# A transformer block with seven-product multiplications: the additions of the heads' raw weight blocks go from GpSimd to VectorE

## The chip, the cores and the metric

One core of a Trainium2 chip. A core has five engines that run their own instruction queues in order: TensorE (PE, the matrix products; its weight loads are listed apart as PEld), VectorE (DVE), ScalarE (ACT), GpSimd (POOL) and SyncE (SP, here only a queue for DMAs). The metric is the time of one execution in microseconds (us) on the device; lower is better.

## What is computed

One layer of a diffusion transformer block for a sequence of 2048 tokens of width 1024, with 256 context tokens. Cut to what matters:

```python
hx = rmsnorm(x, norm1_g) * (1 + sc1) + sh1             # the same for ctx -> hc
p  = hx @ w_in                                         # 1024 x 4608, split into heads of 128 columns:
#   4 gated (HGRN2) heads: query, value, forget gate of both directions, output gate
#   4 retention heads:     query, key (both with a 2d rotary embedding), value, gate
mix = bidirectional chunk scans of the 8 heads, started from the context's states
x  = x + g1 * (mix @ w_out)
hx2 = rmsnorm(x, norm2_g) * (1 + sc2) + sh2
gate, up = split(hx2 @ w_up)                           # 2 x 2816 columns
x  = x + g2 * ((silu(conv3(gate)) * up) @ w_down)
return rmsnorm(x, final_g)
```

## The kernel before

**Products.** All large matrix products are made in float16 pairs: a float32 operand is scaled by a power of two and written as a float16 value and its float16 rest, and three products of TensorE (lines 88 to 90) stand for one. On top of that the products are blocked two by two and made with seven block products instead of eight. For that the operand on the left is turned into seven sums and differences of its four blocks.

**Weights of a head.** `head_weights(h)` (line 692) gives, for each head, two pairs of column groups of `w_in` (for heads 0 to 6: "z" with the gates, or key and query, and "vg" with value and gate; for head 7 the pair "z" alone, since its value and gate are single). Each pair is loaded into two tiles `raw` of 128x8x128 float32. ScalarE squares both (L718) for the scale, a small matrix product sums over the partitions, and a handful of 128x1 instructions of VectorE (L99 to L103, L684 to L689) make a power of two of it. Then `pair_blocks` (line 668) makes the seven blocks: for each one, ScalarE writes the scaled float16 value (L674) and VectorE the rest (L675, which reads that value and the raw block). The blocks beyond the four raw ones come from `left_blocks` (line 511), in place, by four additions or subtractions of 128x512 float32, which this file calls "additions":

```python
        emit(3, a22)
        add(a22, a21, a22, ALU.add)          # line 519
        yield
        emit(4, a22)
        add(a21, a11, a21, ALU.subtract)     # line 522
        yield
        emit(6, a21)
        add(a11, a22, a11, ALU.subtract)     # line 525
        yield
        emit(5, a11)
        add(a12, a12, a11, ALU.subtract)     # line 528
        yield
        emit(2, a12)
```

`emit` is the pair of L674 and L675. `add` is the function handed in by the caller. There are 2 x 7 + 1 = 15 pairs over the eight heads, so 60 additions of this kind, named `raw<-raw` in the profile.

**Two other users.** `up_weights` (line 1494) does the same, by `pair_blocks`, for the 22 pairs of `w_up` (named `wur<-wur`), and `act_pairs` does it for activations, by `left_blocks` directly (`act<-act`).

**What runs beside it.** While one group of 512 tokens of a head goes through its scan (`hg_sweep1`, line 839, for the gated heads; `ret_sweep1`, line 1226, for retention), the projections of the next group are woven in between (`hg_proj`, `ret_proj`). The next head's weights are worked out by a list of items, a few of which are taken up at two points of each group (`tick`). VectorE's large pieces in the scans are the products on K and Q by the running gates (L874, L879; L759 multiplies neighbouring gates) and, for retention, the rotary embedding (L1200, L1222, L1223). GpSimd has, beside the additions, the sum of K over both directions (L824), one half of the rotary product (L1199) and the small reciprocal roots of the norms (L71 to L76). During the first three retention heads the remaining modulation rows are summed up on VectorE as well (`macc`, L301, L303).

**Order of the work.** The program is written as one sequence. A planner orders it when the program is made, with a model of every instruction's duration, and fixes the order in which each engine's queue holds its instructions; semaphores between engines follow from the tiles that are read and written. Nothing is ordered by hand around the additions.

Of the kernel before, what the change touches and what calls it, by code (L numbers as in the profile page):

```python
# [50 lines left out]
def view(t, off, dims):  # L51
    return bass.AP(t.tensor, t.offset + off, [t.ap[0]] + dims)


class Kern:
# [609 lines left out]
        yield  # L665


    def pair_blocks(self, raws, W, s, neg):

        nc = self.nc  # L670

        def emit(m, v):
            sc = neg if m == 3 else s
            nc.scalar.activation(W[m][:, 0], v, AF.Copy, scale=sc)  # L674
            nc.vector.scalar_tensor_tensor(W[m][:, 1], v, sc, W[m][:, 0], ALU.mult, ALU.subtract)  # L675
        blocks = [r[:, 4 * c:4 * c + 4] for r in raws for c in range(2)]
        yield from self.left_blocks(blocks, emit, nc.gpsimd.tensor_tensor)

    def scales(self, total, dqx, tag):

# [11 lines left out]
    def head_weights(self, h):  # L692

        if h < NH:
            want = [("z", "z", (1024 + h * P, 1536 + h * P)), ("q", "q", (h * P,)), ("vg", "vg", (512 + h * P, 2048 + h * P))]
        else:
            o = (h - NH) * P
            want = [("z", "z", (3072 + o, 2560 + o))]
            vg = (3584 + o, 4096 + o)
            want += [("vg", "vg", vg)] if h < 2 * NH - 1 else [("v", "vg", vg[:1]), ("g", "vg", vg[1:])]  # L700
        nc = self.nc
        src = self.I["w_in"][0].rearrange("(k p) n -> p k n", p=P)
        W, items = {}, []
        for nm, tag, cols in want:
            raws, st = [], {}

            def load(cols=cols, raws=raws, tag="ou2" if h == 0 and nm == "q" else "wr"):
                for c in cols:
                    raws.append(self.slot_tile([P, KT, P], F32, tag, "raw"))
                    nc.sync.dma_start(raws[-1], src[:, :, c:c + P])  # L710

            def start(nm=nm, tag=tag, raws=raws, st=st):
                n = len(raws)
                w = [self.slot_tile([P, 2, 4, P], F16, tag, "w_" + nm) for _ in range(7 if n == 2 else 2)]
                ssq = self.kp.tile([P, n], F32, tag=f"ssqw{n}", bufs=2, name="ssqw")
                for i, r in enumerate(raws):
                    junk = w[5 + i if n == 2 else 1].rearrange("p a k t -> p (a k t)")
                    nc.scalar.activation(junk, r.rearrange("p k t -> p (k t)"), AF.Square, scale=4.0 if n == 2 else 1.0,  # L718
                                         accum_out=ssq[:, i:i + 1])
                s, neg, dq = self.scales(self.allsum(ssq), self.dqx[:, 0:1] if h else None, "dq" + nm)  # L720
                W[nm] = w, dq
                if n == 2:
                    st["steps"] = self.pair_blocks(raws, w, s, neg)
                    next(st["steps"])
                else:
                    for c in range(2):
                        v = raws[0][:, 4 * c:4 * c + 4]
                        nc.scalar.activation(w[c][:, 0], v, AF.Copy, scale=s)
                        nc.vector.scalar_tensor_tensor(w[c][:, 1], v, s, w[c][:, 0], ALU.mult, ALU.subtract)

            def more(st=st):
                next(st["steps"], None)
                next(st["steps"], None)
            items.append((load, start))
            if len(cols) == 2:
                items += [(None, more)] * 3
        return W, items
# [756 lines left out]
    def up_weights(self, j, ty):  # L1494

        nc, kp = self.nc, self.kp
        wup = self.I["w_up"][0].rearrange("(k p) n -> p k n", p=P)
        raw = []
        for f in (j, j + NJ):
            r = self.slot_tile([P, KT, P], F32, "wr", "wur")  # L1500
            nc.sync.dma_start(r, wup[:, :, ty * FF + f * P:ty * FF + (f + 1) * P])
            raw.append(r)
        yield
        W = [self.slot_tile([P, 2, 4, P], F16, "z", "w7") for _ in range(7)]
        ssq = kp.tile([P, 2], F32, tag="ssqw2", bufs=2, name="ssqw")
        sqs = [W[5 + i].rearrange("p a k n -> p (a k n)").bitcast(BF16) for i in range(2)]
        for i in range(2):
            nc.scalar.activation(sqs[i], raw[i].rearrange("p k n -> p (k n)"), AF.Square, scale=4.0, accum_out=ssq[:, i:i + 1])
        yield
        col = self.ps("sc", [P, 2], "col")  # L1510
        for i in range(2):
            for k in range(KT):
                nc.tensor.matmul(col[:, i:i + 1], sqs[i][:, k * P:(k + 1) * P], self.onesb, start=k == 0 and i == 0,
                                 stop=k == KT - 1 and i == 1, skip_group_check=True)
        s, neg, dq = self.scales(self.allsum16(ssq, "sc"), self.dqx[:, 1:2], ("dqz", "dqvg")[ty])

        if ty == 0:
            tap = kp.tile([P, 2, 3], F32, tag="taps", bufs=2, name="taps")
            nc.vector.tensor_scalar(tap, view(self.cw, j, [[NJ, 2], [NF, 3]]), dq, None, ALU.mult)
            row = kp.tile([P, 2], F32, tag="row", bufs=2, name="row")  # L1520
            nc.vector.scalar_tensor_tensor(row, col, 1.0 / 16, view(self.a2, j, [[NJ, 2]]), ALU.mult, ALU.mult)
            nc.vector.tensor_tensor(row, row, view(self.c2, j, [[NJ, 2]]), ALU.add)
            self.rows[j] = row
            self.W[j, 0] = W, tap
        else:
            row = self.rows.pop(j)
            q = kp.tile([P, 2], F32, tag="wdq", bufs=4, name="q")
            nc.vector.tensor_scalar(q, col, self.xx, 1.0, ALU.mult, ALU.mult)
            nc.vector.tensor_tensor(q, q, row, ALU.mult)
            nc.vector.tensor_tensor(q[:, 0:1], q[:, 0:1], q[:, 1:2], ALU.max)  # L1530
            sa, ia = self.pow2(kp, q[:, 0:1], 1, "a")
            nc.vector.tensor_copy(self.sas[:, j:j + 1], sa)
            nc.vector.tensor_copy(self.ias[:, j:j + 1], ia)
            self.W[j, 1] = W, dq
        yield

        yield from self.pair_blocks(raw, W, s, neg)

    def down_blocks(self, j):

# [331 lines left out]
```

## Time and profile before

| | |
|---|---|
| median of 3 runs | 2688.24 us (2686.87 to 2689.38) |
| the profiled execution | 2689.31 us; its span from first to last instruction 2687.5 us |
| granted TensorE clock, mean | 0.976 |
| busy: PE, PEld | 2529.3 us (94%), 1666.2 us (62%) |
| busy: DVE, ACT, POOL | 1845.9 us (69%), 1335.7 us (50%), 711.2 us (26%) |
| the 60 additions, on POOL | 93.0 us |

Busy time is the time in which an engine had at least one instruction running. Rows of groups read: line, engine, operation, written tile <- read tiles, shape, count, then busy us and mean ns of one, then the idle time of the engine just before them and what ended it. Rows of stretches (from:to in us) read: length, then for PE, PEld, DVE, ACT and POOL the busy us with the number of instructions, then the granted clock, the DMA share and GB/s. Rows of a timeline read: start, duration, engine, line, operation; instructions of one engine may overlap by a few hundredths of a us, as the next one starts before the end of the last is recorded. Rows of the chain read: start, duration, engine, tile and line.

### The profile page before, as it was taken

To read this page: it belongs to the slowest core of one execution; us is meant where nothing else is said; L and a number is where in the kernel's file an instruction comes from. 1 tells how busy PE (TensorE), PEld (TensorE's weight loads), DVE (VectorE), ACT (ScalarE), POOL (GpSimd) and SP (SyncE) were. 2 spreads that over 40 slices of the span, in tenths; PEclk is the share of its full clock that TensorE was granted. 3 is DMA by queue.
4 is the path that set the end of the run, shared out by engine and by line. 5 is a ranking of instruction groups with operands and counts; after the bars stand their busy time and mean duration, and the time that the engine had idled before them with its cause. 6 is when DMAs were issued, how large, how long until landed. Compare 5 with 4: busy or idle time off the path is not lost.

```text
span 2687.5 us, 56080 instructions
## 1 busy us (share of the span) xinstructions
PE 2529.3 (94%) x22763; PEld 1666.2 (62%) x22763; DVE 1845.9 (69%) x3619; ACT 1335.7 (50%) x2846; POOL 711.2 (26%) x805
## 2 busy tenths in 40 slices
PE   5689999999999999998999899999999999999998
PEld 2578888888889889896444344444444444444443
DVE  4888777776767686666465878888888887323553
ACT  4666456564555444445455556555555555311210
POOL 1201112111223232221334344343443342000102
PEclk7799999999999999999999999999999999999999
DMA  7324334243337575755521223333323325634552
GB/s 273 134 84 158 104 111 139 87 139 119 120 124 260 197 245 182 245 197 179 196 98 48 94 94 114 106 106 114 118 99 106 118 91 205 246 131 186 204 196 94
DMA packets 213620, 393.96 MB, mean 147 GB/s; under 512 B 15600, under 2 KB 97748, under 8 KB 208753
## 3 DMA queue, kind: packets, MB, share of 16 engines
q1 hardware_dynamic: 203808, 373.42, 40.2%
q10 hardware_dynamic: 9248, 16.79, 1.9%
q8 instruction: 178, 2.92, 0.5%
q14 instruction: 82, 0.66, 0.1%
q0 software_dynamic: 304, 0.17, 0.0%
HBM read 298.57 MB, written 91.75 MB: 145 GB/s over the span
## 4 chain that ended last, share of the span: by engine, by line
PE 67%; DVE 15%; issue 6%; ACT 5%; DMA 4%; POOL 3%; SPq 0%; ACTq 0%; DVEq 0%; POOLq 0%
PE pa L88 7%; PE pa L89 7%; PE pa L90 7%; PE pd L88 5%; PE pd L90 5%; PE pd L89 5%; PE pc L88 3%; PE pc L90 3%; PE pc L89 3%; PE pb L88 2%; PE pb L89 2%; PE pb L90 2%; PE opp L90 2%; PE opp L89 2%; PE opp L88 2%
## 5 line engine op out<-in xcount | busy, mean ns | idle before, releaser
L88 PE MATMUL pa<-feat,w 128*128 128x512 f16 x704 | 264.5, 380 | 8.5 <-ACT ta L575 5.6
L89 PE MATMUL pa<-feat,w 128*128 128x512 f16 x704 | 267.5, 380 | 0.0
L90 PE MATMUL pa<-feat,w 128*128 128x512 f16 x704 | 267.0, 380 | 0.0
L89 PE MATMUL pd<-wd,actl 128*128 128x512 f16 x616 | 233.3, 379 | 0.0
L90 PE MATMUL pd<-wd,actl 128*128 128x512 f16 x616 | 233.3, 379 | 0.0
L88 PE MATMUL pd<-wd,actl 128*128 128x512 f16 x616 | 232.6, 379 | 0.0
L89 PEld LDWEIGHTS <-w 128*128 128x128 f16 x1232 | 120.6, 98 | 151.1 <-issue 12.8
L90 PEld LDWEIGHTS <-w 128*128 128x128 f16 x1232 | 120.7, 98 | 146.2 <-issue 1.9
L88 PEld LDWEIGHTS <-w 128*128 128x128 f16 x1232 | 120.6, 98 | 141.7 <-issue 1.8
L89 PEld LDWEIGHTS <-hx 128*128 128x128 f16 x1824 | 182.5, 100 | 10.4 <-issue 8.1
L90 PEld LDWEIGHTS <-hx 128*128 128x128 f16 x1824 | 182.2, 100 | 4.2 <-issue 3.4
L88 PEld LDWEIGHTS <-hx 128*128 128x128 f16 x1824 | 182.3, 100 | 2.1
L1622 ACT ACTIVATE st<-act,modT 128x512 f16<-128x512 f32 x154 | 107.2, 717 | 109.5 <-DVE act L1612 63.0
L1623 DVE SCALAR_TENSOR_TENSOR st<-act,modT,st 128x512 f16<-128x512 f32 x154 | 141.3, 952 | 29.5 <-ACT st L1622 28.8
L88 PE MATMUL pa<-w_vg,hx 128*128 128x128 f16 x800 | 145.7, 223 | 0.3
L90 PE MATMUL pa<-w_vg,hx 128*128 128x128 f16 x800 | 145.7, 222 | 0.0
L89 PE MATMUL pa<-w_vg,hx 128*128 128x128 f16 x800 | 145.7, 223 | 0.0
L88 PE MATMUL pc<-feat,w 128*128 128x512 f16 x352 | 134.1, 381 | 2.2 <-ACT feat L1397 1.2
L89 PEld LDWEIGHTS <-w_z 128*128 128x128 f16 x1072 | 107.5, 100 | 44.3 <-issue 33.4
L89 PE MATMUL pc<-feat,w 128*128 128x512 f16 x352 | 134.2, 381 | 0.1
L90 PE MATMUL pc<-feat,w 128*128 128x512 f16 x352 | 134.2, 381 | 0.0
L88 PE MATMUL pa<-hx,w_z 128*128 128x256 f16 x464 | 126.6, 273 | 5.4 <-DVE rV L617 4.1
(547 smaller groups left out, 7466.8 us busy)
## 6 DMA issues: line engine op xcount, KB each, us to landing
hx<-hxd SPq DMA_DIRECT2D x212, 512.0 KB, 4.8
actd<-st SPq DMA_DIRECT2D x154, 256.0 KB, 2.0
actl<-actd SPq DMA_DIRECT2D x28, 1024.0 KB, 5.0
wur<-in_w_up_dram SPq DMA_DIRECT2D x44, 512.0 KB, 3.8
raw<-in_w_in_dram SPq DMA_DIRECT2D x36, 512.0 KB, 4.6
wm<-in_w_mod_dram SPq DMA_DIRECT2D x64, 256.0 KB, 3.9
hxd<-hx SPq DMA_DIRECT2D x28, 512.0 KB, 3.6
wdb<-in_w_down_dram SPq DMA_DIRECT2D x44, 256.0 KB, 4.1
```

The source lines that it names most:

```text
L88: mm(ps, lhs(0), rhs(0), start=start, stop=False, skip_group_check=True)
L89: mm(ps, lhs(0), rhs(1), start=False, stop=False, skip_group_check=True)
L90: mm(ps, lhs(1), rhs(0), start=False, stop=stop, skip_group_check=True)
L1622: nc.scalar.activation(p[:, 0], v, AF.Copy, scale=s)
L1623: nc.vector.scalar_tensor_tensor(p[:, 1], v, s, p[:, 0], ALU.mult, ALU.subtract)
```

## The change

`pair_blocks` gets one argument more, the engine of the additions. `head_weights` hands in VectorE, `up_weights` hands in GpSimd as before. The 60 additions on `raw` move to VectorE; the 88 on `wur` and the 88 on `act` stay. Their order in the program's sequence, their operands and their shapes are the same.

```diff
-    def pair_blocks(self, raws, W, s, neg):
+    def pair_blocks(self, raws, W, s, neg, eng):
...
         blocks = [r[:, 4 * c:4 * c + 4] for r in raws for c in range(2)]
-        yield from self.left_blocks(blocks, emit, nc.gpsimd.tensor_tensor)
+        yield from self.left_blocks(blocks, emit, eng.tensor_tensor)
...
                 if n == 2:
-                    st["steps"] = self.pair_blocks(raws, w, s, neg)
+                    st["steps"] = self.pair_blocks(raws, w, s, neg, nc.vector)
                     next(st["steps"])
...
-        yield from self.pair_blocks(raw, W, s, neg)
+        yield from self.pair_blocks(raw, W, s, neg, nc.gpsimd)
```

## The prediction, made before the changed kernel was run

> **What bounds the kernel now.** I read the page first, for the balance of the engines and the chain that ends last.
>
> ```profile
> PE 2529.3 (94%) x22763; PEld 1666.2 (62%) x22763; DVE 1845.9 (69%) x3619; ACT 1335.7 (50%) x2846; POOL 711.2 (26%) x805
> PE 67%; DVE 15%; issue 6%; ACT 5%; DMA 4%; POOL 3%; SPq 0%; ACTq 0%; DVEq 0%; POOLq 0%
> ```
>
> TensorE is busy 94% of the span, so all that the other engines can give back is part of its idle time. Next, the busy time by stage: the first 134 us are the start, 134 to 1206 us the eight heads in full swing.
>
> ```profile
> 0.00:134.00 134.00, 82.81 (x655) 56.72 (x656) 88.19 (x211) 79.93 (x167) 30.97 (x48) 0.76 0.58 204
> 134.00:1206.00 1072.00, 1006.23 (x14731) 924.07 (x14729) 774.79 (x1676) 574.08 (x1416) 232.80 (x251) 0.98 0.47 157
> ```
>
> The columns are length, then busy time of PE, PEld, DVE, ACT, POOL. In the heads PE is idle for 1072 - 1006.2 = 65.8 us (6.1%). VectorE is at 72% on average, and the question is where. The additions come in 15 groups of four (two groups a head, one for the last). I laid a window round each group, from 3 us before its first addition to 5 us after its last. The first two, a quiet one, the last, and the sum of all 15:
>
> ```profile
> 41.80:55.20 13.40, 6.24 (x24) 4.11 (x24) 12.82 (x31) 8.92 (x15) 5.19 (x4) 0.50 0.01 4
> 78.80:92.30 13.50, 12.34 (x133) 10.99 (x132) 13.38 (x20) 12.54 (x24) 7.96 (x9) 1.00 0.15 45
> 826.50:840.50 14.00, 13.23 (x181) 12.54 (x179) 12.74 (x19) 5.66 (x12) 10.38 (x8) 1.00 0.66 203
> 1065.00:1079.30 14.30, 11.85 (x152) 10.79 (x150) 13.99 (x19) 6.39 (x13) 9.28 (x5) 1.00 0.57 191
> sum 223.50, PE 184.33 PEld 163.83 DVE 216.26 ACT 132.42 POOL 128.60; mean PE 12.29 PEld 10.92 DVE 14.42 ACT 8.83 POOL 8.57
> ```
>
> Here VectorE is full: 216.3 of 223.5 us, 97%. The 13 windows of the heads (the sum less the first two) hold 196.6 us with PE busy 165.8: idle 30.8 us, 15.7%. Outside them PE is idle 34.9 of 875.4 us, 4.0%. At that rate the 13 windows would have lost 7.9 us, so 23 us of PE idle time, 1.77 a group, belong to the neighbourhood of the additions. That is the stake.
>
> **Why VectorE is full there.** The timeline of one group, VectorE first, then GpSimd:
>
> ```profile
> 415.84 1.77 DVE L879 TENSOR_TENSOR Q<-Q,T 128x512 f32<-128x512 f32 x1
> 417.86 1.43 DVE L759 TENSOR_TENSOR T<-FG 128x512 f32<-128x512 f32 x1
> 419.33 1.65 DVE L874 TENSOR_TENSOR K<-K,T 128x512 f32<-128x512 f32 x1
> 420.89 1.75 DVE L675 SCALAR_TENSOR_TENSOR w_vg<-raw,p2s,w_vg 128x512 f16<-128x512 f32 x1
> 422.57 0.68 DVE L874 TENSOR_TENSOR K<-K,T 128x512 f32<-128x512 f32 x1
> 423.17 0.68 DVE L879 TENSOR_TENSOR Q<-Q,T 128x512 f32<-128x512 f32 x1
> 423.77 0.74 DVE L675 SCALAR_TENSOR_TENSOR w_vg<-raw,p2s,w_vg 128x512 f16<-128x512 f32 x1
> 415.32 1.73 POOL L519 TENSOR_TENSOR raw<-raw 128x512 f32<-128x512 f32 x1 [1.47 <-DVE w_vg L675]
> 417.14 1.61 POOL L522 TENSOR_TENSOR raw<-raw 128x512 f32<-128x512 f32 x1
> 418.82 1.60 POOL L525 TENSOR_TENSOR raw<-raw 128x512 f32<-128x512 f32 x1
> 420.50 1.59 POOL L528 TENSOR_TENSOR raw<-raw 128x512 f32<-128x512 f32 x1
> ```
>
> The same product on Q takes 1.77 us while an addition runs on GpSimd and 0.68 us after the last one has ended; the conversion L675 takes 1.75 against 0.74. Against the quick rows (0.68 for the three products, 0.74 for the conversion) the four cost 1.09 + 0.75 + 0.97 + 1.01 = 3.8 us more. Each ends only after the addition that it overlapped: 415.32 + 1.73 = 417.05, and the product, begun at 415.84, ends at 417.61. VectorE is held up once per GpSimd addition, for most of it. The Trainium skill, page "SBUF — State Buffer", section "Who interferes with whom", states this as a rule: the two engines share one pair of ports as an exclusive lock, and the second to issue stands still until the first is through, if VectorE has two SBUF inputs or a two-port mode; the trace agrees in these rows (1.77 against 0.68 us).
>
> I counted all VectorE instructions that overlap one of the 60 additions and exceed the lower quartile of their own form by over 0.06 us: 62 of them, together 53.1 us too long. The first and the last:
>
> ```profile
> 45.40 0.71 DVE L353 TENSOR_SCALAR A<-modu,p2s 128x16 f32<-128x16 f32 x1
> 1073.30 2.11 DVE L1200 TENSOR_TENSOR Q<-K,sin 64x1024 f32<-64x1024 f32 x1
> ```
>
> **The change, part by part.** One edit: four operations in each of 15 groups change engine; no DMA, no tile and no semaphore by hand is touched. GpSimd loses these rows (the two below them stay):
>
> ```profile
> L525 POOL TENSOR_TENSOR raw<-raw 128x512 f32<-128x512 f32 x15 | 24.8, 1651 | 1.2
> L522 POOL TENSOR_TENSOR raw<-raw 128x512 f32<-128x512 f32 x15 | 23.4, 1562 | 1.2
> L528 POOL TENSOR_TENSOR raw<-raw 128x512 f32<-128x512 f32 x15 | 23.4, 1561 | 0.9
> L519 POOL TENSOR_TENSOR raw<-raw 128x512 f32<-128x512 f32 x15 | 21.4, 1425 | 215.8 <-DVE w_z L675 157.5 <-DVE w_vg L675 36.9 <-DVE p2t L100 19.9
> L1199 POOL TENSOR_TENSOR Q<-K,sin 64x1024 f32<-64x1024 f32 x16 | 51.4, 3214 | 160.7 <-ACT K L615 160.4
> L824 POOL TENSOR_TENSOR ks<-K 128x512 f32<-128x512 f32 x16 | 25.5, 1592 | 179.2 <-DVE K L820 78.5 <-PE sc L863 63.7 <-ACT w_vg L718 29.0
> ```
>
> That is 21.4 + 23.4 + 24.8 + 23.4 = 93.0 us of GpSimd, which is idle 74% of the span; by itself it is worth nothing.
>
> VectorE gains 60 additions of 128x512 f32. Rows at 422.57 to 423.77 above: such an instruction shows 0.68 us, and the next starts 0.60 us later, so 60 x 0.60 = 36.1 us of its queue (60 x 0.68 = 40.8 us in the busy column). VectorE loses the 53.1 us of standing still. Net -17.0 us, -1.13 a group, in stretches where it is full. The busy column should go from 1845.9 to 1845.9 + 40.8 - 53.1 = 1833.6.
>
> What that is worth on the path: followed back, the chain that ends last runs along VectorE through 12 of the 15 groups, on the very instructions that stand still, as in the group shown:
>
> ```profile
> 415.92 1.68 DVE Q L879
> 417.94 1.36 DVE T L759
> 419.33 1.65 DVE K L874
> 420.97 1.67 DVE w_vg L675
> ```
>
> In those 12, 45.3 of the 53.1 us were counted, against 12 x 2.41 = 28.9 us to be paid: -16.4 us. In the other three (the windows at 826.5, 945.1 and 1065.0) it runs through the first two additions themselves, as in the last of them:
>
> ```profile
> 1068.03 1.28 POOL raw L519
> 1069.30 0.07 issue
> 1069.37 1.61 POOL raw L522
> 1070.98 0.02 issue
> 1071.01 0.73 ACT w_z L674
> ```
>
> There 1.28 + 1.61 = 2.9 us become 2 x 0.68 = 1.4 us: -1.5 us each, -4.5 us. Together -20.9 us on the chain. TensorE must be able to use it: a window cannot give more than its PE idle time above the 4% found elsewhere. The window at 826.5 has 14.00 - 13.23 = 0.77 us of idle time and gives almost nothing, the one at 1065.0 has 2.45 and gives its full 1.5. Taken window by window this leaves -15.7 us as the upper end. The lower end of the gain is nothing.
>
> Two effects are not in the rows of before. First, GpSimd's two remaining kinds (3.2 and 1.6 us, above) still hold up VectorE, 16 times each, unchanged: cost 0, since each holds up whichever VectorE instruction meets it, an addition as well as another. Second, the order of each queue is worked out by a planner when the program is made; with 60 more entries for VectorE it may place its other work differently anywhere in the heads. Nothing shows its size; by the idle time of PE outside the windows (34.9 us over 875 us), a tenth either way is +-3.5 us. ScalarE's conversions, which read the sums, get them earlier if VectorE is on time (0.68 instead of 1.4 to 1.65 us each); I count nothing for it. After the heads PE is the bound or the work is unchanged, so what is gained is kept.
>
> I take six tenths of -15.7, that is -9.4 us: nearer to the chain's rows, which show the loss directly, than to nothing, with an allowance for the queue's new order. The profiled execution took 2689.3 us (span 2687.5), 1.1 above the median of 2688.2 of the three runs; 2688.2 - 9.4 = 2678.8, say 2679 us.
>
> **The rivals.**
>
> *No change that can be measured.* The runs before spread over 2.5 us; about 5.4 us, 0.2%, is what a measurement of this kernel can tell from no change. For it: TensorE is 94% busy, and a window such as 826.5 has nothing to give; if only a third of -15.7 comes through, that is -5: 2683 to 2688 us. Against it: 15.7% idle in the windows, 4.0% outside.
>
> *Slower: VectorE's queue waits for ScalarE between the additions.* On GpSimd the four additions ran ahead, whatever VectorE was doing. In VectorE's queue they stand in order, with the conversions L675 that need ScalarE's L674 (0.73 us above) on their results. If the planner sets addition and conversion back to back, VectorE waits for ScalarE four times a group: 4 x 0.73 = 2.9 us less the 1.13 saved, +1.8 us a group, +27 us in all, 2715; at six tenths +16, 2704 us. It decides once more than 1.13 us a group of such waiting is exposed. Against it, conversion after ScalarE exists already, and the rows show what VectorE idles for it (last field) and how much it stands still:
>
> ```profile
> L675 DVE SCALAR_TENSOR_TENSOR w_z<-raw,p2s,w_z 128x512 f16<-128x512 f32 x48 | 44.9, 952 | 1.4 <-ACT w_z L674 1.4
> L675 DVE SCALAR_TENSOR_TENSOR w_vg<-raw,p2s,w_vg 128x512 f16<-128x512 f32 x42 | 36.7, 888 | 4.3 <-ACT w_vg L674 4.3
> L675 DVE SCALAR_TENSOR_TENSOR w_z<-raw,neg,w_z 128x512 f16<-128x512 f32 x8 | 5.9, 740 | 0.0
> ```
>
> 5.7 us over 90 conversions, 0.4 us a group: the planner finds other work in between. (952 against the 740 of the conversions that come before any addition is the standing still once more.) The plainer form of this rival, that a full engine gets 36.1 us more, needs the 53.1 us not to come back; the quick rows at 422.57 to 423.77 speak against that. The Trainium skill, "Perfetto Trace Analysis", section "Optimizing Scalar/DVE Operations", would send work the other way, off a saturated VectorE, GpSimd included, but adds that between these two it might not help because of the shared port; the 53.1 us lost for 93.0 us of GpSimd work agree with the addition.
>
> **How the numbers follow.** Faster as worked out 0.52 (own range 2670 to 2683); no change 0.28; slower 0.20. The first two alone would span 2670 to about 2694. The upper bound of the gain, -15.7, and the planner's 3.5 give a low end of 2668; part of the slower case must be in, so the high end is 2696. By the bound of 0.2%: faster 0.51, same 0.28, slower 0.21.
>
> **What would show it.** Right: GpSimd at 618 us and VectorE at about 1834; 60 rows of about 0.68 us on VectorE at L519 to L528; L675 on raw blocks at 740 to 800 ns; PE's idle time in the heads down from 65.8 to some 55 us. Wrong: additions of 1 us or more (held up by the rope product), ScalarE's idle time before L674 or VectorE's before L675 grown by over 10 us, or the windows' PE idle time unchanged with VectorE no longer full, which would mean that something else held TensorE.

## The result, and the profile after

The changed kernel takes 2642.9 us (median of 4 runs, 2640.4 to 2644.5) against 2688.7 us before on the same chip: 45.8 us less, a ratio of 0.983 (95% interval 0.982 to 0.984). The forecast was 2679 us, with 2668 to 2696 as its range. The direction was right, but the forecast gain of 9.4 us is a fifth of what came, and the time lies below the range.

The profiled execution has a span of 2642.5 us, 45.0 less than before. First the page's row of busy times, then the stages: rows of before, up to the second store of a head's output, from there to the last of them (the end of the heads), and the rest, and the same three of after.

```profile
PE 2513.3 (95%) x22763; PEld 1658.3 (63%) x22763; DVE 1825.8 (69%) x3679; ACT 1333.9 (50%) x2846; POOL 624.5 (24%) x745
```

```profile
0.00:382.40 382.40, 310.54 (x4339) 260.90 (x4339) 282.80 (x669) 229.65 (x521) 69.71 (x84) 0.90 0.43 149
382.40:1281.30 898.90, 841.07 (x11691) 768.88 (x11678) 628.18 (x1365) 463.49 (x1163) 205.20 (x245) 0.98 0.51 168
1281.30:2687.50 1406.20, 1377.71 (x6754) 636.40 (x6752) 934.89 (x1586) 642.54 (x1163) 436.24 (x476) 0.99 0.38 132
```

```profile
0.00:360.10 360.10, 298.66 (x4264) 252.31 (x4265) 271.44 (x679) 225.08 (x510) 43.06 (x64) 0.91 0.44 154
360.10:1239.40 879.30, 837.80 (x11744) 768.64 (x11744) 620.23 (x1416) 466.92 (x1175) 143.19 (x205) 0.99 0.52 174
1239.40:2642.50 1403.10, 1376.85 (x6757) 637.36 (x6755) 934.15 (x1586) 641.86 (x1163) 438.30 (x476) 0.99 0.37 132
```

The heads end 41.9 us sooner: 382.4 - 360.1 = 22.3 in the first stretch, 19.6 in the second. After them only 3.1 us differ. Over the whole span TensorE's idle time went from 2687.5 - 2529.3 = 158.2 to 2642.5 - 2513.3 = 129.2 us, 29.0 less, and its busy time fell by 16.0 us, with the same 22763 matmuls. I had not reckoned with the second part at all.

VectorE's rows of the additions and of the conversions of raw blocks:

```profile
L519 DVE TENSOR_TENSOR raw<-raw 128x512 f32<-128x512 f32 x15 | 10.2, 681 | 0.0
L522 DVE TENSOR_TENSOR raw<-raw 128x512 f32<-128x512 f32 x15 | 11.1, 742 | 0.0
L525 DVE TENSOR_TENSOR raw<-raw 128x512 f32<-128x512 f32 x15 | 10.2, 681 | 0.0
L528 DVE TENSOR_TENSOR raw<-raw 128x512 f32<-128x512 f32 x15 | 14.4, 957 | 0.0
L675 DVE SCALAR_TENSOR_TENSOR w_z<-raw,p2s,w_z 128x512 f16<-128x512 f32 x48 | 37.1, 785 | 0.1
L675 DVE SCALAR_TENSOR_TENSOR w_vg<-raw,p2s,w_vg 128x512 f16<-128x512 f32 x42 | 32.0, 769 | 6.2 <-ACT w_vg L674 6.2
```

An addition takes 0.68 us, but for three (1.59, 2.78 and 2.77 us) that meet one of GpSimd's remaining operations. The conversions fell from 952 and 888 to 785 and 769 ns. The group whose timeline was shown in the prediction now reads, on VectorE alone:

```profile
398.71 0.68 DVE L519 TENSOR_TENSOR raw<-raw 128x512 f32<-128x512 f32 x1
399.31 0.68 DVE L759 TENSOR_TENSOR T<-FG 128x512 f32<-128x512 f32 x1
399.91 0.68 DVE L522 TENSOR_TENSOR raw<-raw 128x512 f32<-128x512 f32 x1
400.51 0.69 DVE L874 TENSOR_TENSOR K<-K,T 128x512 f32<-128x512 f32 x1
401.12 0.74 DVE L675 SCALAR_TENSOR_TENSOR w_vg<-raw,p2s,w_vg 128x512 f16<-128x512 f32 x1
401.78 0.68 DVE L874 TENSOR_TENSOR K<-K,T 128x512 f32<-128x512 f32 x1
402.38 0.69 DVE L525 TENSOR_TENSOR raw<-raw 128x512 f32<-128x512 f32 x1
402.98 0.68 DVE L879 TENSOR_TENSOR Q<-Q,T 128x512 f32<-128x512 f32 x1
```

Every instruction has its quick duration and the next starts 0.60 us later (0.66 after a conversion); the additions stand scattered among the others.

Windows round the 15 groups, laid by the same rule as before: the one of this group, and the sum of all.

```profile
395.70:410.30 14.60, 14.60 (x198) 12.80 (x197) 13.37 (x28) 11.22 (x27) 0.00 (x0) 1.00 0.59 172
sum 239.50, PE 215.71 PEld 195.52 DVE 229.47 ACT 155.51 POOL 37.50; mean PE 14.38 PEld 13.03 DVE 15.30 ACT 10.37 POOL 2.50
```

TensorE's idle time in them went from 223.5 - 184.3 = 39.2 to 239.5 - 215.7 = 23.8 us: 15.4 less. So the windows gave about what the prediction held to be the upper end (15.7); the other 13.6 us of idle time went outside them, and the 16.0 us of busy time was in no sum of mine. VectorE is still busy for 229.5 of the 239.5 us, 96%, without the standing still.

### The profile page after: what moved, and what is told of

Read it like the earlier page. It is cut to its first block, busy times and chain, and to the rows that moved or that the text cites. A ratio compares the mean times of both kernels' runs of the same rounds, so it can differ in the third digit from the quotient of the medians.

```text
span 2642.5 us, 56066 instructions
## 1 busy us (share of the span) xinstructions
PE 2513.3 (95%) x22763; PEld 1658.3 (63%) x22763; DVE 1825.8 (69%) x3679; ACT 1333.9 (50%) x2846; POOL 624.5 (24%) x745
## 4 chain that ended last, share of the span: by engine, by line
PE 70%; DVE 14%; ACT 5%; DMA 4%; issue 4%; POOL 2%; SPq 0%; DVEq 0%; ACTq 0%; POOLq 0%
PE pa L88 8%; PE pa L89 7%; PE pa L90 7%; PE pd L90 5%; PE pd L88 5%; PE pd L89 5%; PE pc L88 4%; PE pc L89 3%; PE pc L90 3%; PE pb L88 2%; PE pb L90 2%; PE pb L89 2%; PE opp L89 2%; PE opp L88 2%; PE opp L90 2%
## 5 line engine op out<-in xcount | busy, mean ns | idle before, releaser
L89 PEld LDWEIGHTS <-hx 128*128 128x128 f16 x1824 | 179.9, 99 | 5.5 <-issue 3.4
L90 PEld LDWEIGHTS <-hx 128*128 128x128 f16 x1824 | 179.8, 99 | 3.1 <-issue 2.4
L88 PEld LDWEIGHTS <-hx 128*128 128x128 f16 x1824 | 180.2, 99 | 2.1
L88 PE MATMUL pa<-w_vg,hx 128*128 128x128 f16 x800 | 142.7, 220 | 0.2
L89 PE MATMUL pa<-w_vg,hx 128*128 128x128 f16 x800 | 142.4, 219 | 0.0
L90 PE MATMUL pa<-w_vg,hx 128*128 128x128 f16 x800 | 142.3, 219 | 0.0
```

What stands on the lines that cost most here:

```text
L88: mm(ps, lhs(0), rhs(0), start=start, stop=False, skip_group_check=True)
L89: mm(ps, lhs(0), rhs(1), start=False, stop=False, skip_group_check=True)
L90: mm(ps, lhs(1), rhs(0), start=False, stop=stop, skip_group_check=True)
```

## The experiments

After the result three theories stood. A: VectorE stands still behind GpSimd's additions, and that cost far more, set against the additions' own price, than I took it for. B: the gain comes from the planner's new order of all queues, which differs widely between the two kernels. C: on GpSimd the sums come late, and the chain of weights is longer for it. Differences of time are between medians; each kernel was timed beside runs of the kernel before on its chip.

| kernel | us | before beside it | ratio to before (95%) |
|---|---|---|---|
| the changed kernel | 2642.9 | 2688.7 | 0.983 (0.982 to 0.984) |
| e1_first_head | 2685.0 | 2693.0 | 0.997 (0.996 to 0.998) |
| e2_later_heads | 2655.6 | 2693.0 | 0.987 (0.985 to 0.989) |
| e3_spare_sums | 2691.9 | 2693.0 | 1.000 (0.999 to 1.001) |
| e4_spare_memsets | 2643.9 | 2693.0 | 0.981 (0.980 to 0.983) |
| e5_short_gpsimd | 2645.7 | 2691.3 | 0.983 (0.981 to 0.984) |
| e6_twice_on_vector | 2676.1 | 2691.3 | 0.994 (0.993 to 0.996) |
| e7_heads_off_gpsimd | 2651.2 | 2691.3 | 0.985 (0.984 to 0.987) |
| e8_upward_too | 2648.7 | 2691.3 | 0.984 (0.983 to 0.986) |
| e9_late_sums | 2664.2 | 2692.5 | 0.990 (0.988 to 0.991) |
| e10_spare_scalings | 2664.2 | 2692.5 | 0.990 (0.988 to 0.991) |
| e11_ks_vector | 2651.3 | 2692.5 | 0.985 (0.984 to 0.987) |
| e12_short_others | 2630.5 | 2690.3 | 0.977 (0.975 to 0.979) |

**The change for a part of the heads.**

```diff
-                    st["steps"] = self.pair_blocks(raws, w, s, neg, nc.vector)
+                    st["steps"] = self.pair_blocks(raws, w, s, neg, nc.gpsimd if h else nc.vector)   # e1_first_head
+                    st["steps"] = self.pair_blocks(raws, w, s, neg, nc.vector if h else nc.gpsimd)   # e2_later_heads
```

> Additions on VectorE for head 0 only (8 of 60), on GpSimd for heads 1 to 7. Theory A (VectorE stands still behind GpSimd's additions; each of the 15 groups gives back its part of the 45 us): only the two groups of the start give back, 4 to 8 us: 2681 to 2685 us. Theory B (the gain is the planner's new order of the queues, not the engine of the additions): the gain does not go by groups; by 360 us the changed kernel was already 22 us ahead, so 15 to 25 us may come from the new order of the start alone: 2664 to 2674 us.

> The opposite: additions on GpSimd for head 0, on VectorE for heads 1 to 7 (52 of 60). Theory A: the rest of the gain, 37 to 41 us: 2648 to 2652 us. Theory B: what the start's order gave is lost, 20 to 30 us remain: 2659 to 2669 us.

Measured: 8.0 and 37.4 us less than before. Together 45.4, the whole of the change. The two groups of the start give 4 us each, the 13 later ones 2.9 each. That is theory A's additive gain: both gains lie in its ranges (4 to 8 and 37 to 41 us), while the second time, 2655.6 us, is 3.6 above the range given, as the kernel before took 2693.0 us here. The new order of the start alone is not worth 15 us.

**GpSimd's load put back, read and written.** Both have the additions on VectorE.

```diff
-        yield from self.left_blocks(blocks, emit, eng.tensor_tensor)
+        def add(o, x, y, op):
+            eng.tensor_tensor(o, x, y, op)
+            if eng is nc.vector:
+                spare = self.ep.tile([P, G], F32, tag="spare", bufs=1, name="spare")
+                nc.gpsimd.tensor_tensor(spare.rearrange("p (k t) -> p k t", t=P), o, o, ALU.add)   # e3_spare_sums
...
+                nc.gpsimd.tensor_tensor(spare[:, :1], o[:, 0, :1], o[:, 0, :1], ALU.add)           # e4_spare_memsets
+                for _ in range(2):
+                    nc.gpsimd.memset(spare, 0.0)
+        yield from self.left_blocks(blocks, emit, add)
```

> The changed kernel with GpSimd's load put back: after each addition on VectorE, GpSimd adds the result to itself into a spare tile of 128x512 that nobody reads. Theory A: VectorE stands still again for some 50 us and keeps the 41 us of additions: at least as slow as before, 2688 to 2715 us. Theory B, and theory C (what counts is that a sum is there after 0.7 instead of 1.3 to 1.7 us): nobody waits for the spare sums, 2643 to 2655 us.

> Control for the kernel with spare sums: GpSimd writes zeros into the spare tile (two memsets of 128x512 after each addition, behind an addition of one column), so it is busy but reads almost nothing. TensorE's queue holds the same order as in the changed kernel. Theory A with standing still caused by reads alone: 2640 to 2648 us, as the changed kernel. If any GpSimd instruction holds VectorE up, written only or not: 2660 us or more. Theory B: as the changed kernel.

GpSimd's and VectorE's rows of the kernel with spare sums, then its busy times up to the end of the heads:

```profile
L681 POOL TENSOR_TENSOR spare<-raw 128x512 f32<-128x512 f32 x60 | 84.3, 1406 | 241.5 <-DVE raw L678 203.5 <-DVE p2t L101 20.7 <-issue 8.4
L678 DVE TENSOR_TENSOR raw<-raw 128x512 f32<-128x512 f32 x60 | 52.9, 882 | 0.0
L675 DVE SCALAR_TENSOR_TENSOR w_z<-raw,p2s,w_z 128x512 f16<-128x512 f32 x48 | 49.3, 1038 | 0.1
0.00:1279.40 1279.40, 1146.30 (x16010) 1027.68 (x16011) 934.33 (x2094) 691.49 (x1683) 266.54 (x329) 0.96 0.49 163
```

The same of the kernel with memsets:

```profile
L683 POOL MEMSET spare<- 128x512 f32 x120 | 64.3, 536 | 6.5 <-POOL spare L681 0.2
0.00:1237.80 1237.80, 1131.93 (x16007) 1016.91 (x16008) 891.66 (x2094) 692.62 (x1683) 282.13 (x449) 0.97 0.51 168
```

From here on an overlong instruction of VectorE is put down to the GpSimd operation that it overlaps longest. That gives 51.9 us for the kernel before, where the prediction's count of any overlap gave 53.1. GpSimd works more in the second kernel (282 against 267 us), but what it does is almost all writing, and VectorE is held up for 2.3 us only: 2643.9 us, as the changed kernel. With spare sums VectorE stands still for 44.8 us again (51.7 by the prediction's count), the conversions into `w_z` take 1038 ns, and the whole gain is gone: 48.0 us slower than with memsets, on the same chip.

Nothing waits for the spare sums: no instruction uses them, and each load that fills a `raw` tile again starts at least 0.6 us after the last spare sum that had ended, but within 0.4 us of a ScalarE or VectorE instruction on `raw`. So theory C is not needed for the loss: GpSimd is no link of the chain of weights here, and what is late is late because VectorE stands still. Theory B, by which the order alone makes the time, had forecast 2643 to 2655 us. The pair also prices standing still: 48.0 us by 44.8 or 51.7, about 0.9 to 1.1 us of the end for each.

**A shorter read on GpSimd, near the changed kernel's order.**

```diff
+        self.spare = ep.tile([P, G], F32, name="spare")
+        nc.gpsimd.memset(self.spare, 0.0)
...
+                nc.gpsimd.tensor_tensor(spare[:, :1], o[:, 0, :1], o[:, 0, :1], ALU.add)
+                nc.gpsimd.tensor_scalar(spare, spare, 0.5, 0.25, ALU.mult, ALU.add)
```

> As the kernel with spare sums, but GpSimd scales a spare tile of 128x512 in place (one input, read from the on-chip memory) behind an addition of one column, and the order of TensorE's queue is all but that of the changed kernel (289 of 36482 places differ; with spare sums 2057). Theory A: VectorE stands still in proportion to the scaling's length; at the price of about 1 us each, between 10 us (if a scaling takes 0.5 us) and 48 us (if it takes as long as a sum) slower than the changed kernel: 2653 to 2690 us. Theory B (order): 2643 to 2648 us.

```profile
L684 POOL TENSOR_SCALAR spare<-spare 128x512 f32<-128x512 f32 x60 | 68.5, 1141 | 5.0
0.00:1255.60 1255.60, 1145.31 (x16007) 1028.85 (x16008) 907.43 (x2094) 692.72 (x1683) 282.16 (x390) 0.96 0.50 166
```

One read instead of two, and 14.3 us of standing still, 13.8 of it behind the scalings. By the ratios it is (0.990 - 0.983) x 2690, some 18 us slower than the changed kernel, with TensorE's queue in all but the same order. So these 18 us do not come from the order; 1.3 us for each is somewhat above the price of the spare sums.

**Additions on GpSimd, but short; and twice on VectorE.** The first kernel leaves out seven eighths of every sum.

```diff
+            n = 16 if eng is nc.vector else P                                                       # e5_short_gpsimd
+            nc.gpsimd.tensor_tensor(o[:, :, :n], x[:, :, :n], y[:, :, :n], op)
...
+            if eng is nc.vector:                                                                    # e6_twice_on_vector
+                spare = self.ep.tile([P, G], F32, tag="spare", bufs=1, name="spare")
+                nc.vector.tensor_tensor(spare.rearrange("p (k t) -> p k t", t=P), o, o, ALU.add)
```

> Additions on GpSimd as before, but each over 16 of its 128 columns in each of the 4 sub-blocks (64 of 512 elements; the rest of each sum is left out). VectorE neither pays for additions nor stands still for long. Theory A (standing still is what cost): some 40 to 46 of the 53 us of standing still go, at the price of about 1 us each that the spare sums showed: 2636 to 2650 us. Theory B (VectorE as the engine of the additions matters through the planner's order): nearer to before, 2670 to 2690 us.

> The changed kernel with a second addition of 128x512 on VectorE after each of the 60 (into a spare tile that nobody reads): 36 us more in VectorE's queue, in the same stretches, and no more contention. If VectorE's own work there costs its full length, as the prediction had it: 2643 + 36 = 2679 us. If only standing still costs and the planner finds room for planned work (the spare sums on GpSimd left about 0.2 us per us): 2647 to 2657 us.

The short additions on GpSimd, then the stretch up to the end of the heads, with short additions and with twice on VectorE:

```profile
L679 POOL TENSOR_TENSOR raw<-raw 128x64 f32<-128x64 f32 x60 | 36.7, 611 | 199.3 <-DVE w_z L675 159.7 <-DVE p2t L100 22.5 <-DVE w_vg L675 13.6
0.00:1235.60 1235.60, 1143.42 (x16010) 1025.39 (x16011) 858.07 (x2034) 690.50 (x1683) 214.35 (x329) 0.96 0.51 169
0.00:1262.00 1262.00, 1141.72 (x16010) 1024.03 (x16011) 928.13 (x2154) 694.46 (x1685) 190.44 (x269) 0.96 0.50 165
```

With short additions GpSimd still does 60 of them, VectorE stands still for 3.4 us behind them instead of 52, and has no additions to do. It gains 45.6 us, no more than the changed kernel, which does all 60 on VectorE; and 4945 of TensorE's 22763 matmuls stand in another place than there, so an order as different as that need not change the time. With every addition done twice, the second set costs (0.994 - 0.983) x 2690, some 30 us for 36 us of work: my expectation from the spare sums was wrong, the prediction's full price nearly right. Four kernels now make a square:

| | additions not on VectorE | additions on VectorE |
|---|---|---|
| VectorE not held up | 2645.7 (short on GpSimd) | 2642.9 (changed), 2643.9 (memsets) |
| held up, 45 to 52 us | 2690 to 2693 (before) | 2691.9 (spare sums) |

Down a column, standing still costs 46 to 48 us. In the right column VectorE's own work is the same in all three kernels; in the left one the sums also come sooner, in 0.61 instead of some 1.5 us. Along a row, the 36 us of additions cost nothing that can be told from the noise. The busy times say where they go: between short additions and the changed kernel VectorE's work up to the end of the heads rises from 858.1 to 271.44 + 620.23 = 891.7 us, and its idle time falls from 377.5 to 347.7. Up to that load planned work falls into idle time; beyond it (928.1, idle 333.9) most of it does not.

**Sums held back.**

```diff
+                nc.gpsimd.tensor_tensor(spare[:, :1], o[:, 0, :1], o[:, 0, :1], ALU.add)
+                nc.gpsimd.memset(spare, 0.0)
+                nc.gpsimd.tensor_tensor(o[:, 0, :1], o[:, 0, :1], spare[:, :1], ALU.add)
```

> The changed kernel with each sum held back on GpSimd without much reading: after the addition on VectorE, GpSimd adds one column, writes zeros over a spare tile (0.54 us) and adds zero to one column of the sum in place, so that the next addition and the conversions wait for it, about as long as for GpSimd's additions before. Theory C (part of the 45 us is that sums come late): 2660 to 2675 us. Theory A (standing still alone): 2643 to 2652 us.

```profile
0.00:1261.00 1261.00, 1144.82 (x16015) 1026.09 (x16016) 887.97 (x2095) 690.98 (x1683) 279.02 (x449) 0.96 0.50 165
```

It lands in theory C's range: about 18 us slower than the changed kernel by the ratios, with VectorE no busier (888.0 us) but idle for 373.0 instead of 347.7. Lateness can cost, then, where the next addition stands in VectorE's own queue. It does not show that lateness cost the kernel before anything: there the additions stood in GpSimd's queue, and the spare sums bring the whole loss back without anything waiting for GpSimd. How much of the 45 us lateness would have cost alone stays open.

**GpSimd's other work.**

```diff
-        nc.gpsimd.tensor_tensor(ks, K[:, 0], K[:, 1], ALU.add)
+        nc.vector.tensor_tensor(ks, K[:, 0], K[:, 1], ALU.add)                                      # e7, e11
...
-        nc.gpsimd.tensor_tensor(pt[64:], qk[:64], sines[:64], ALU.mult)
+        nc.vector.tensor_tensor(pt[64:], qk[:64], sines[:64], ALU.mult)                             # e7
...
-        yield from self.pair_blocks(raw, W, s, neg, nc.gpsimd)
+        yield from self.pair_blocks(raw, W, s, neg, nc.vector)                                      # e8
```

> The changed kernel with the two other large GpSimd operations of the heads, the sum of K (16 of 128x512) and the half rotary product (16 of 64x1024), on VectorE too. They hold VectorE up for 13.4 + 18.5 = 32 us in the changed kernel and cost it 16 x 0.6 + 16 x 1.15 = 28 us. Theory A with a price of about 1 for standing still and 0.2 to 0.3 for planned work: 20 to 28 us faster, 2615 to 2625 us. If VectorE's work costs its full length: 2635 to 2645 us.

> The changed kernel with the 16 sums of K on VectorE too (the rotary product stays on GpSimd): 13.4 us of standing still go, 16 x 0.6 = 9.6 us of additions come. Standing still at about 0.9 and planned work between 0 and 0.7 per us: 5 to 12 us faster than the changed kernel, 2631 to 2638 us. If the changed kernel is at the floor that TensorE sets: 2640 to 2646 us.

> The changed kernel with the 88 additions of the upward weights on VectorE as well. There TensorE is idle for less than 1 us in most stretches of 73 us, so there is nothing to give back except at the stage's first pair: 2638 to 2645 us. If standing still cost there as in the heads (56 us counted): 2600 us or less. If VectorE, at 80% in that stage, becomes the bound: over 2650 us.

None beats the changed kernel: 0.985, 0.985 and 0.984 against 0.983, with intervals that touch or overlap. In the upward stage taking away the 56 us of standing still (counted in the kernel before) gains nothing, as expected, since TensorE has next to no idle time there; the 2648.7 us are still 3.7 above the range that was given. In the heads the first two were expected faster, by any of their ranges, and are not. The last run bears on why. It leaves out seven eighths of both results:

```diff
+        nc.gpsimd.memset(ks, 0.0)
+        nc.gpsimd.tensor_tensor(ks[:, :64], K[:, 0, :64], K[:, 1, :64], ALU.add)
...
+        nc.gpsimd.memset(pt[64:], 0.0)
+        nc.gpsimd.tensor_tensor(pt[64:, :, :64], qk[:64, :, :64], sines[:64, :, :64], ALU.mult)
```

> The changed kernel with GpSimd's two other operations cut to an eighth of their columns (the sum of K over 64 of 512, the half rotary product over 64 of 512 in both halves; the rest is filled with zeros by GpSimd, which reads nothing). Some 25 of the 32 us of standing still that are left go, and VectorE gets no work for it. If standing still costs about 0.9 per us here as well: 20 to 25 us faster than the changed kernel, 2618 to 2626 us, and the two kernels that moved these operations to VectorE paid it back with the work. If VectorE no longer sets the time at these places: 2636 to 2646 us.

```profile
0.00:1229.10 1229.10, 1133.46 (x16015) 1019.61 (x16016) 863.47 (x2094) 691.80 (x1683) 153.28 (x301) 0.97 0.51 169
```

Standing still behind these two goes from 31.9 to 1.8 us, and the time falls by (0.983 - 0.977) x 2690, some 16 us, between the two ranges: about 0.5 us for each. The two results also come sooner, so not all of the 16 us need be due to standing still. There is something left to gain, but the kernel that moves both operations to VectorE gives it back for 28 us of work, at nearly the price that the second set of additions had.

## Why the prediction was right in sign and wrong in size

- *VectorE is full round the additions because it stands still.* That standing still there is what cost the time was right: put back by spare sums it undoes the whole gain, put back in part by scalings it undoes 18 us. Fullness itself was a poor sign: after the change VectorE is as full in the windows (96% against 97%), with work that can be placed.
- *Durations.* Right: additions at 0.68 us, GpSimd at 624.5 us (618 forecast), VectorE at 1825.8 (1834).
- *"60 x 0.60 = 36.1 us of its queue", charged at full against the 53.1 us.* This step failed. On the chain I paid 28.9 of 45.3 us for the additions; the square shows that they cost nothing that can be told from the noise (2642.9 us with them, 2645.7 without). I took a unit of planned work and a unit of standing still as equal, because the windows were full. But the planner spreads planned work: the additions of a group now stand scattered, and VectorE's idle time up to the end of the heads fell from 370.3 us (1281.3 - 282.8 - 628.2) to 347.7. At 0.9 us for each of some 52 us of standing still, the low end of the price of the spare sums, and nothing for the additions, the sum would have been -47. That price was known only after the result, and it is no constant: the runs gave 0.5 to 1.3.
- *"A window cannot give more than its PE idle time above the 4% found elsewhere."* The windows gave 15.4 us, near the 15.7, but that was no limit for the kernel. TensorE's idle time fell by another 13.6 us outside them, and its busy time fell by 16.0. That what was late in the windows made other work late is the likely reason for the first; no run here shows it by itself. In the heads, from 134 us to 75.3 us before their end, the idle time fell from 65.8 to 1030.1 - 987.6 = 42.5 us, where the prediction had said some 55. The sum itself was off as well: by the rule as it is stated, the 15 windows leave 18.1 of the 20.9 us, not 15.7.
- *The busy time.* The prediction had no term for it. In one of the groups of the kernel before, TensorE runs at half clock after an idle stretch (TensorE's columns come first, the granted clock third from the end; then the matmuls that end the wait):

```profile
367.90:371.30 3.40, 0.00 (x0) 0.00 (x0) 3.40 (x5) 1.85 (x4) 3.40 (x3) 0.95 0.92 293
371.00:374.40 3.40, 3.07 (x56) 3.01 (x57) 3.40 (x6) 1.47 (x2) 3.15 (x5) 0.50 0.16 61
374.40:377.80 3.40, 3.40 (x75) 3.04 (x73) 3.40 (x9) 0.51 (x1) 0.35 (x1) 1.00 0.68 211
371.33 0.65 PE L863 MATMUL sc<-Q,Kl 128*32 128x32 f32 x32 [3.44 <-DVE Q L879]
```

  TensorE waits for 3.44 us, until VectorE's product on Q is through, which takes 1.75 instead of 0.68 us beside one of GpSimd's additions; it then runs for 3.4 us at a clock of 0.50. The Trainium skill, page "TensorE: Matmul & The Clock Gate", section "Part 1: The HAM clock gate (the "warmup" mystery)", states this: half rate after an idle window of about 3.4 us, full rate after a busy one; the trace agrees in these rows, and the last section has a row where half clock follows a shorter wait. Summed over the clock's records, the time lost to half clock fell from 65.3 to 52.4 us. Only 41.1 and 32.1 us of this were lost while TensorE was busy, so the clock accounts for 9.0 of the 16.0 us; where the other 7.0 went stays open. The mean granted clock went from 0.976 to 0.981.
- *"I take six tenths."* With the limit this turned -20.9 on the chain into -9.4. The chain's reading was the better one, and the allowance for the queue's order went the wrong way: the kernels that part the causes leave no more than a few us to the order. That the sign came out right owes nothing to luck; that the windows' 15.4 us came so near to 15.7 does, as two terms of that sum were off.
- *The rivals.* VectorE's waiting for ScalarE hardly grew: its idle time before L675 is 0.1 + 6.2 us, after 1.4 + 4.3. The form in which a full engine gets 36 us more and slows down is what the second set of additions shows, but only from the second set on.

## What to carry to other kernels

Time in which an engine is held up in the middle of an instruction and planned work are not the same currency: planned work may fall into idle time (the first 36 us of it here, hardly the second), standing still stops everything that is queued behind. To price a shared resource, put the load back where nobody waits for it (a spare result), and set beside it the same load without the contention (a write alone). And an idle limit taken from windows round the cause is no limit for the gain, where lateness may travel on and where TensorE's clock can fall after a wait.

## What the runs showed of the hardware that I had not expected

- GpSimd holds VectorE up when it reads, and not when it only writes: 120 memsets of 128x512 (64.3 us), each pair behind a sum of one column, held VectorE up for 2.3 us and cost no time, 60 sums of 128x512 (84.3 us) held it up for 44.8 us, 60 scalings of one input (68.5 us) for 13.8.
- Half clock can also follow a wait of less than 3.4 us. In the kernel before, TensorE is idle for 1.8 us, and busy for 1.6 of the 3.4 us from 1009.3 us on; then 27 matmuls run in the 3.4 us at half clock, and 42 in the next 3.4. Waits of 2.0 and 2.1 us, to 958.7 and 1078.8 us, were not followed by half clock; what decides it stays open:

```profile
1009.30:1011.10 1.80, 0.04 (x1) 0.00 (x0) 1.80 (x2) 0.17 (x1) 1.27 (x1) 1.00 0.96 347
1012.70:1016.10 3.40, 3.40 (x27) 3.34 (x27) 0.75 (x1) 1.60 (x5) 0.00 (x0) 0.50 0.54 204
1016.10:1019.50 3.40, 3.40 (x42) 3.34 (x41) 0.42 (x1) 1.94 (x8) 1.60 (x4) 1.00 0.67 216
```
